# One more sevenfold pair in each of the last two down passes, twice three sevens in a row, and four more weight sums made ahead

## The chip, the cores and the metric

The kernel runs on one core of one Trainium2 chip. The time is device microseconds of one launch; lower is better. The core's engines work from queues of their own and hand over by semaphores: PE (TensorE, matmuls, with its weight loads listed as PEld), DVE (VectorE), ACT (ScalarE), POOL (GpSimd, here almost only an issuer of DMAs), SP (SyncE, an issuer of DMAs).

## The reference, cut to what matters

One decoder layer in float32 for 256 tokens of width 2048: a norm, an RG-LRU branch and a windowed attention branch side by side, gates that merge them, an output projection, and an MLP of width 8192. The change touches the MLP's down projection:

```python
D_MODEL, SEQ, D_FF = 2048, 256, 8192
def rmsnorm(x, g):
    return x * rsqrt(mean(x * x) + 1e-6) * g
# x is the sum of the input and the normed mixer output
u = square(relu(rmsnorm(x, g_mlp_pre) @ w_mlp_up))     # (256, 8192)
y = u @ w_mlp_down                                     # (256, 2048)
out = x + rmsnorm(y, g_mlp_post)
```

## The kernel before, in words

**Products.** PE multiplies in a format (fp32r) that holds less than float32, so each weight and each activation is split into a high part and a low rest. ACT casts (`whi<-wraw`, L108), DVE subtracts (`wlo<-wraw,whi`, L109), and every product is three matmuls, high by high, high by low, low by high (`product`, L1204).

**Weight stream.** All weights come through one stream (class `Stream`). A weight chunk is two halves of 128 x 1024; raw halves are loaded by SP into four slots (five in the MLP, `xraw`), and split into six slots of high and low halves, up to six halves ahead of PE (`AHEAD`). So ACT and DVE work ahead until a slot is missing that PE must free.

**The MLP.** It runs in two halves f = 0, 1 of 4096 inner channels each: an up stage (16 steps), then two down passes n = 0, 1, for the left and the right 1024 output columns. A down pass goes through 16 pairs p of K-blocks. A *plain* pair takes 8 products, so 24 matmuls of 512 columns. A *sevenfold* pair (Strassen's scheme, list `SEVENS`) takes 7, so 21, and in exchange needs sums of weight blocks, T1, T3 and T4, and sums of activation blocks (made once for f, when the up stage hands its block on, four more DVE operations for a pair). The three T sums are split like weights: three casts of 512 columns on ACT (L154, `thi`) and three subtractions on DVE (L155, `tlo`), into three slots each.

**Where the sums come from.** For most sevenfold pairs DVE makes them on the spot from the raw halves (`right_sums`, three operations, L59, L61 and L62, into `t`; they overwrite part of the raw half). For the pairs of `SUMMED` they are made ahead, in earlier stages (`sums_ahead`): POOL loads the chunk in four DMAs of 256 KB (`early<-in_w_dn`, L365), DVE adds, POOL stores the results in three DMAs to a DRAM buffer (`away<-`, L374). In the pass POOL then fetches the three pieces in three DMAs of 256 KB (`second<-away`, L138) into a pool of four slots, and SP loads the raw second half from the DRAM buffer. `gaps` spaces the generator's steps: one step is taken at each half or pair that PE begins.

**The order around it.** Pairs of `SUMS_FIRST` run their three T products first, others last. The T parts of a pair are put into ACT's and DVE's queues one sevenfold pair later than its halves. The pass of f = 1, n = 1 ends with the folds of the output; it has a gain `g3` to multiply into the accumulators, in `between(p)`, four operations of 512 columns. In the pass f = 1, n = 0 the last sevenfold pair's banks are folded into tiles `t` after its products (L1253 to L1257), and the pass ends with four folds `acc<-d..,t` (L1374), which wait for PE.

Of the kernel before, what the change touches and what calls it, by code (L numbers as in the profile page):

```python
# [35 lines left out]

WRAW, WHALF, T2, HELD = 4, 6, 8, 4

SEVENS = (0, 1, 3, 4, 6, 7, 9, 10, 12, 13), (0, 1, 3, 4, 6, 7, 9, 10, 12)
SUMMED = (4, 7, 10, 13), (4, 7, 10)  # L40
SUMS_FIRST = (0, 3, 6, 9, 12)
PAIRS = 16


# [160 lines left out]
def layer(tc, x, few, kx_first, kx_rest, pos_row, gains, w_q, w_xy, w_rg, w_g, w_rp, w_ap, w_out,  # L205
# [155 lines left out]
    def sums_ahead(c, gaps, rooms):  # L361

        w = flat(unit("early", F32))
        for i in range(4):
            nc.gpsimd.dma_start(w[:, quarter(i)], chunks[c][:, quarter(i)])  # L365
            for _ in range(gaps[0]):
                yield
        for _ in range(gaps[1]):
            yield
        one, two = rooms()  # L370
        right_sums(nc.vector, w[:, 0:1024], w[:, 1024:2048], one, two)
        to, b = ws.summed[c]
        for away, of in ((b, w[:, 1024:2048]), (to[:, 0:1024], one), (to[:, 1024:1536], two)):
            nc.gpsimd.dma_start(away, of)  # L374
            for _ in range(gaps[2]):
                yield
# [508 lines left out]
    for m in range(4):  # L885
        recur(m)
        if m == 0:
            pump(99)
            ctx_ps.close()
            psg = ctx1.enter_context(tc.tile_pool(name="psg", bufs=2, space=bass.MemoryType.PSUM))  # L890
            pairs.append(ctx1.enter_context(tc.tile_pool(name="psa2", bufs=1, space=bass.MemoryType.PSUM)))
        if m < 2:
            for i in range(2):
                attn_proj(2 * m + i)
        if m < 3:
            gates(m)
# [24 lines left out]

    ahead = [g_rnn()]
    gates(3)
    ws.side += [sums_ahead(c, (1, 3, 1), unit_rooms) for c in summed[:6]]
    ahead.append(g_rnn())
    for n in range(4):
        gs = ahead.pop(0)
# [193 lines left out]
    for tb in range(TB):  # L1121
        for i in range(2):
            q = 2 + i
# [93 lines left out]
    def down(f, n, uT, held, order, finish, early, between=lambda p: None, behind=lambda: None, closing=False):  # L1217

        two = [pair(f"s{i}") for i in range(2)]
        banks = {name: two[i // 2][:, i % 2].rearrange("p a b -> p (a b)")  # L1220
                 for i, name in enumerate(("P1", "P6", "Q5", "N7"))}
        banks.update((name, bank(psb, f"d{name}")) for name in ("P2", "Q3", "Q4", "Cs"))
        begun = set()
        v = nc.vector

        def step(p, i, hi, lo, name, at=0, w=512, into=None):
            tb, n2 = name
            b = into or PLACE[name]
            o = 0 if into else at
            t = slice(tb * P, tb * P + P)  # L1230
            c = slice(n2 * 512 + at, n2 * 512 + at + w)
            a = uT[p][:, i]
            product(banks[b][:, o : o + w], (a[:, 0, t], a[:, 1, t]), (hi[:, c], lo[:, c]), b in begun,
                    p == PAIRS - 1 and i == 1, w < 512 and not into)
            begun.add(b)

        ready = {}
        for p in range(PAIRS - held - closing):
            if p in SEVENS[f]:
                parts = ws.seven()  # L1240
                names = list(LEFT)
                names.sort(key=lambda name: ("T1", "T3", "T4").index(LEFT[name][1]) if LEFT[name][1] in ("T1", "T3", "T4")
                           else 9 if p in SUMS_FIRST else -1)
                for name in names:
                    i, w = LEFT[name]
                    product(banks[name], left(uT[p], i), parts[w], name in begun,
                            p == SEVENS[f][-1] and (name in ("P1", "P6", "Q5", "N7") or closing and name == PLACE[order[-1]]))
                    begun.add(name)
                if p == SEVENS[f][-1]:
                    for name in ((1, 0), (0, 0), (1, 1), (0, 1)):  # L1250
                        ready[name] = u2("t")
                    x = ready[0, 0]
                    nc.scalar.copy(ready[1, 0], banks["P1"])  # L1253
                    v.tensor_tensor(x, banks["P6"], ready[1, 0], ALU.add)
                    v.tensor_tensor(ready[1, 1], banks["Q5"], x, ALU.subtract)
                    v.tensor_tensor(x, x, banks["N7"], ALU.subtract)
                    v.tensor_tensor(ready[0, 1], ready[1, 1], banks["N7"], ALU.add)  # L1257
                    early(ready)
            else:
                for i in range(2):  # L1260
                    hi, lo = ws.half()
                    for name in order:
                        step(p, i, hi, lo, name)
            between(p)
        parts = []
        if closing:
            for i in range(2):
                parts.append((PAIRS - held - 1, i) + ws.half())
                for name in order[:2]:
                    step(*parts[i], name)  # L1270
        first = len(parts)
        parts += [(p, i) + ws.half(False) for p in range(PAIRS - held, PAIRS) for i in range(2)]
        behind()
        begun.discard("P1")
        for k, name in enumerate(order):
            todo = parts[first if k < 2 else 0 :]
            b, t = banks[PLACE[name]], ready[name]
            if closing and k == 1:
                a, r = order[-1], slice(256, 512)
                fold = lambda: pin(v.tensor_tensor(ready[a][:, r], banks[PLACE[a]][:, r], ready[a][:, r], ALU.add))  # L1280
                for e in todo:
                    step(*e, name)
                finish(name, b, t, 0, 512, fold)
            elif closing and k == 3:
                for e in todo:
                    step(*e, name, 0, 256)
                finish(name, b, t, 0, 256)
                for e in todo:
                    step(*e, name, 256, 256, "P1")
                finish(name, banks["P1"], t, 256, 256)  # L1290
            else:
                for e in todo:
                    step(*e, name)
                finish(name, b, t, 0, 512)
        ws.ahead(ws.at - 1)

    for f in range(2):
        uT = {}
        rooms = []
        if f:  # L1300
            ws.side += [sums_ahead(c, (1, 5, 1), ws.sums_rooms) for c in summed[10:]]
        full = []
        for p in range(PAIRS):
            u = u2("u")
            if f == 0 and p == 1:
                ws.side += [sums_ahead(c, (1, 4, 1), lambda: ws.sums_rooms()) for c in summed[6:10]]
            if f == 0 and p < 2:
                up_pair(p, wide(u))
            else:
                a_pair(h2T, wide(u), PRIO if p == PAIRS - 1 else 0)  # L1310
            full.append((p, u))
            if f == 0 and p == R2_AT:
                pump(99)
                spread_r2()
                ctx3.close()
                pc = ctx2.enter_context(tc.tile_pool(name="pc", bufs=1))
                ws.room = u2
                ws.more = lambda: pc.tile([P, 1024], F32, tag="xraw", name="xraw")
                ws.sums_room = lambda tag: pc.tile([P, 512], F32R, tag=tag, bufs=3, name=tag)
                ws.sums_rooms = lambda: [pc.tile([P, n], F32, tag=f"t{n}", name=f"t{n}") for n in (1024, 512)]  # L1320
            if f == 1 or p >= R2_AT:
                for q, u in full:
                    if q % 2 == 0:
                        rooms.append(unit(f"uT{f}{q}"))
                    room = rooms[-1][:, 2 * (q % 2) : 2 * (q % 2) + 2]
                    if q in SEVENS[f]:
                        three = pc.tile([P, 2, 3, P], F32R, tag="three", bufs=len(SEVENS[0]), name=f"three{f}{q}")
                        uT[q] = three, flat(room).rearrange("p (a b c) -> p a b c", a=2, b=4)
                    else:
                        uT[q] = room  # L1330
                    evacuate(f, q, u, uT[q])
                full.clear()
# [26 lines left out]
        def between(p):  # L1359
            if p < 4:  # L1360
                c = quarter(p)
                nc.sync.dma_start(g3[:, c], gains[3][c].partition_broadcast(P))
            if p in (2, 5, 8, 11):
                tb, q = divmod(p // 3, 2)
                c = quarter(q)
                nc.vector.tensor_tensor(acc[tb][:, c], acc[tb][:, c], g3[:, c], ALU.mult)

# [121 lines left out]
```

## Time and profile before

| what | us |
|---|---|
| median of 3 runs (lowest, highest) | 1488.99 (1488.8, 1489.45) |
| the profiled execution's own time | 1488.93 |
| its span | 1487.0 |
| PE busy | 1477.6 (99%) |
| DVE busy | 1144.4 (77%) |
| ACT busy | 854.8 (57%) |
| POOL busy | 77.5 (5%) |

The span is what the trace covers; the time of a run is 1.9 us longer than it. Busy shares are means over stages with different limits. In the trace the second half's up stage lies at about 1139 to 1317 us, its first down pass at 1317 to 1398 and its second at 1398 to 1480. A wait that the views name by a tile and a line is put down to the operation that released it.

### The profile page before, as it was taken

The page shows a single profiled execution, that of the slowest core. Times are in us where ns is not written, and L with a number is a line of the kernel's source. Part 1 is how long each engine was busy: PE and PEld are TensorE (multiplying, and loading weights), DVE is VectorE, ACT ScalarE, POOL GpSimd, SP SyncE. Part 2 cuts the span into 40 slices and gives each one's busy share as a digit, 9 for nine tenths or more (in the row PEclk, how much of TensorE's full clock was granted, in tenths as well). Part 3 has the DMA queues.
Part 4 walks back from the last instruction along what each step waited for, and adds up shares of the span by engine and source line. Part 5 has one row for each costly group of instructions (what it writes and reads, how often), then busy time and mean ns, then how long its engine had stood idle before and what let it go on. Part 6 is the DMA issues. An engine that isn't in the chain of part 4 may idle for free.

```text
span 1487.0 us, 20528 instructions
## 1 busy us (share of the span) xinstructions
PE 1477.6 (99%) x7556; PEld 1253.4 (84%) x7556; DVE 1144.4 (77%) x1503; ACT 854.8 (57%) x1236; POOL 77.5 (5%) x149
## 2 busy tenths in 40 slices
PE   9999999999999999999999999999999999999997
PEld 8887788888889888888889888888888888888886
DVE  6676668759668867665767888798997777699997
ACT  8564565647467665444355665566564545566563
POOL 0000000000000001110000111000111110000000
PEclk9999999999999999999999999999999999999999
DMA  9654543455646567887864987567788686587674
GB/s 342 229 167 143 174 167 135 171 193 174 208 156 214 185 222 249 310 285 244 310 227 162 321 298 272 181 244 252 268 286 307 225 286 222 200 287 251 198 274 171
DMA packets 96902, 342.38 MB, mean 230 GB/s; under 512 B 11553, under 2 KB 11809, under 8 KB 95777
## 3 DMA queue, kind: packets, MB, share of 16 engines
q1 hardware_dynamic: 80352, 288.89, 57.3%
q0 software_dynamic: 12992, 44.05, 8.4%
q10 hardware_dynamic: 3456, 8.13, 1.5%
q8 instruction: 59, 0.97, 0.3%
q14 instruction: 43, 0.34, 0.1%
HBM read 316.38 MB, written 24.64 MB: 229 GB/s over the span
## 4 chain that ended last, share of the span: by engine, by line
PE 97%; DVE 1%; ACT 1%; DMA 0%; issue 0%; DVEq 0%; ACTq 0%
PE ps L296 22%; PE ps L294 11%; PE dQ L1204 8%; PE s L1204 7%; PE dP L1204 4%; PE g L334 4%; PE g L336 4%; PE pp L334 4%; PE g L338 4%; PE pp L336 4%; PE pp L338 4%; PE dCs L1204 2%; PE q L334 2%; PE q L338 2%; PE q L336 2%; PE o L336 2%
## 5 line engine op out<-in xcount | busy, mean ns | idle before, releaser
L109 DVE TENSOR_TENSOR wlo<-wraw,whi 128x1024 fp32r<-128x1024 f32 x469 | 566.6, 1220 | 245.4 <-ACT whi L108 242.9
L108 ACT CAST whi<-wraw 128x1024 fp32r<-128x1024 f32 x469 | 489.9, 1051 | 452.4 <-PE ps L296 92.9
L296 PE MATMUL ps<-h2T,whi 128*128 128x512 f32 x960 | 223.9, 390 | 0.0
L296 PEld LDWEIGHTS ps<-h2T,whi 128*128 128x128 f32 x960 | 178.2, 188 | 35.7
L294 PEld LDWEIGHTS ps<-h2T,wlo 128*128 128x128 f32 x960 | 119.1, 192 | 2.3
L296 PE MATMUL ps<-hT,whi 128*128 128x512 f32 x512 | 120.6, 391 | 0.0
L294 PE MATMUL ps<-h2T,wlo 128*128 128x256 f32 x960 | 119.9, 283 | 0.0
L296 PEld LDWEIGHTS ps<-hT,whi 128*128 128x128 f32 x512 | 94.7, 188 | 19.5 <-issue 0.7
L1204 PE MATMUL dQ<-whi,uT 128*128 128x512 f32 (+1 forms) x284 | 104.1, 385 | 0.0
L334 PE MATMUL g<-whi,hT 128*128 128x512 f32 x256 | 101.0, 395 | 0.0
L338 PE MATMUL g<-whi,hT 128*128 128x512 f32 x256 | 99.7, 389 | 0.0
L336 PE MATMUL g<-wlo,hT 128*128 128x512 f32 x256 | 99.7, 389 | 0.0
L108 ACT CAST whi<-xraw 128x1024 fp32r<-128x1024 f32 x47 | 49.4, 1052 | 40.7 <-PE ps L296 18.4
L109 DVE TENSOR_TENSOR wlo<-xraw,whi 128x1024 fp32r<-128x1024 f32 x47 | 57.3, 1219 | 12.1 <-ACT whi L108 11.2
L294 PEld LDWEIGHTS ps<-hT,wlo 128*128 128x128 f32 x512 | 63.7, 191 | 2.1 <-issue 0.8
L294 PE MATMUL ps<-hT,wlo 128*128 128x256 f32 x512 | 64.6, 283 | 0.0
L365 POOL DMA_DIRECT2D early<-in_w_dn x56 | 30.4, 543 | 651.9 <-DVE px L324 497.6
L1204 PEld LDWEIGHTS dQ<-whi,uT 128*128 128x128 f32 x284 | 53.0, 188 | 10.6
L334 PEld LDWEIGHTS g<-whi,hT 128*128 128x128 f32 x256 | 48.1, 188 | 10.5 <-issue 1.0
L338 PEld LDWEIGHTS g<-whi,hT 128*128 128x128 f32 x256 | 48.0, 188 | 10.2
L336 PEld LDWEIGHTS g<-wlo,hT 128*128 128x128 f32 x256 | 48.1, 188 | 9.4
L1204 PE MATMUL dQ<-wlo,uT 128*128 128x512 f32 (+1 forms) x142 | 54.6, 385 | 0.0
(309 smaller groups left out, 2744.9 us busy)
## 6 DMA issues: line engine op xcount, KB each, us to landing
wraw<-in_w_up SPq DMA_DIRECT2D x106, 512.0 KB, 4.5
wraw<-in_w_dn SPq DMA_DIRECT2D x93, 512.0 KB, 5.0
wraw<-in_w_g SPq DMA_DIRECT2D x64, 512.0 KB, 4.7
wraw<-in_w_xy SPq DMA_DIRECT2D x64, 512.0 KB, 3.9
wraw<-in_w_q SPq DMA_DIRECT2D x32, 512.0 KB, 4.1
wraw<-in_w_ap SPq DMA_DIRECT2D x32, 512.0 KB, 3.9
wraw<-in_w_rp SPq DMA_DIRECT2D x32, 512.0 KB, 5.3
wraw<-in_w_out SPq DMA_DIRECT2D x32, 512.0 KB, 4.4
```

The costliest lines, as they stand in the source:

```text
L108: self.pin(self.nc.scalar.copy(hi, src))
L109: self.latest_low = self.pin(self.nc.vector.tensor_tensor(lo, src, hi.bitcast(F32), ALU.subtract))
L294: mm(ps[:, f, 1, :], w, a[:, 0, :], start=False, stop=j == 1 and k == 7)
L296: mm(ps[:, f].rearrange("p a b -> p (a b)"), w, a.rearrange("p a b -> p (a b)"), start=kt == 0, stop=j == 3 and k == 7)
L334: mm(banks[tb][n], a[:, 0, t], hi[:, n * 512 : n * 512 + 512], start=first, stop=False)
L336: mm(banks[tb][n], a[:, 0, t], lo[:, n * 512 : n * 512 + 512], start=False, stop=False)
L338: mm(banks[tb][n], a[:, 1, t], hi[:, n * 512 : n * 512 + 512], start=False, stop=last)
L365: nc.gpsimd.dma_start(w[:, quarter(i)], chunks[c][:, quarter(i)])
L1204: mm(b, a[x], w[y], start=not begun and i == 0, stop=tail and i == 2, skip_group_check=shared)
```

## The change

In the second half (f = 1) both passes get ten sevenfold pairs, not nine: 0, 1, 3, 4, 5, 7, 8, 9, 11, 12, so that 3-4-5 and 7-8-9 stand in a row, where before no more than two did. Of them 4, 5, 8, 9 and 12 take sums made ahead (before: 4, 7, 10), and 0, 3, 7 and 11 run their T products first. So 18 chunks have sums made ahead, not 14. The first two are made at the attention projections, the next six where six were made before (beside the recurrence's projections), five in the first half's up stage (before four) and five in the second half's up stage (before four), with shorter gaps between the steps. The four multiplies by `g3` are taken at p = 2, 6, 6 and 10 (before 2, 5, 8 and 11). The host's layout of the weight follows `SEVENS`. The program has 6 matmuls fewer, 16 more operations of two tensors on DVE, 7 more casts on ACT, 40 more DMAs on POOL, and as many DMAs on SP as before.

```diff
--- before.py
+++ after.py
@@ -36,9 +36,9 @@
 
 WRAW, WHALF, T2, HELD = 4, 6, 8, 4
 
-SEVENS = (0, 1, 3, 4, 6, 7, 9, 10, 12, 13), (0, 1, 3, 4, 6, 7, 9, 10, 12)
-SUMMED = (4, 7, 10, 13), (4, 7, 10)
-SUMS_FIRST = (0, 3, 6, 9, 12)
+SEVENS = (0, 1, 3, 4, 6, 7, 9, 10, 12, 13), (0, 1, 3, 4, 5, 7, 8, 9, 11, 12)
+SUMMED = (4, 7, 10, 13), (4, 5, 8, 9, 12)
+SUMS_FIRST = (0, 3, 6, 9, 12), (0, 3, 7, 11)
 PAIRS = 16
 
 
@@ -890,6 +890,7 @@
             psg = ctx1.enter_context(tc.tile_pool(name="psg", bufs=2, space=bass.MemoryType.PSUM))
             pairs.append(ctx1.enter_context(tc.tile_pool(name="psa2", bufs=1, space=bass.MemoryType.PSUM)))
         if m < 2:
+            ws.side.append(sums_ahead(summed[m], (2, 3, 1), unit_rooms))
             for i in range(2):
                 attn_proj(2 * m + i)
         if m < 3:
@@ -921,7 +922,7 @@
 
     ahead = [g_rnn()]
     gates(3)
-    ws.side += [sums_ahead(c, (1, 3, 1), unit_rooms) for c in summed[:6]]
+    ws.side += [sums_ahead(c, (1, 3, 1), unit_rooms) for c in summed[2:8]]
     ahead.append(g_rnn())
     for n in range(4):
         gs = ahead.pop(0)
@@ -1240,7 +1241,7 @@
                 parts = ws.seven()
                 names = list(LEFT)
                 names.sort(key=lambda name: ("T1", "T3", "T4").index(LEFT[name][1]) if LEFT[name][1] in ("T1", "T3", "T4")
-                           else 9 if p in SUMS_FIRST else -1)
+                           else 9 if p in SUMS_FIRST[f] else -1)
                 for name in names:
                     i, w = LEFT[name]
                     product(banks[name], left(uT[p], i), parts[w], name in begun,
@@ -1298,12 +1299,12 @@
         uT = {}
         rooms = []
         if f:
-            ws.side += [sums_ahead(c, (1, 5, 1), ws.sums_rooms) for c in summed[10:]]
+            ws.side += [sums_ahead(c, (1, 3, 1), ws.sums_rooms) for c in summed[13:]]
         full = []
         for p in range(PAIRS):
             u = u2("u")
             if f == 0 and p == 1:
-                ws.side += [sums_ahead(c, (1, 4, 1), lambda: ws.sums_rooms()) for c in summed[6:10]]
+                ws.side += [sums_ahead(c, (1, 3, 1), lambda: ws.sums_rooms()) for c in summed[8:13]]
             if f == 0 and p < 2:
                 up_pair(p, wide(u))
             else:
@@ -1360,8 +1361,8 @@
             if p < 4:
                 c = quarter(p)
                 nc.sync.dma_start(g3[:, c], gains[3][c].partition_broadcast(P))
-            if p in (2, 5, 8, 11):
-                tb, q = divmod(p // 3, 2)
+            for k in {2: (0,), 6: (1, 2), 10: (3,)}.get(p, ()):
+                tb, q = divmod(k, 2)
                 c = quarter(q)
                 nc.vector.tensor_tensor(acc[tb][:, c], acc[tb][:, c], g3[:, c], ALU.mult)
```

How the instructions stand now. First DVE in the pass f = 1, n = 0, from the T parts of pair 4 on; halves 474 and 475 are pair 5's, 476 and 477 pair 6's, 478 and 479 pair 7's. Before:

```order
L109 TENSOR_TENSOR wlo475_12066<-xraw_11980,whi475_12065 128x1024
L155 TENSOR_TENSOR tlo_12093<-second_12017,thi_12092 128x512
L155 TENSOR_TENSOR tlo_12097<-second_12018,thi_12096 128x512
L155 TENSOR_TENSOR tlo_12101<-second_12019,thi_12100 128x512
L59 TENSOR_TENSOR t1024_12104<-wraw477_12031,wraw476_11982 128x1024
L61 TENSOR_TENSOR wraw477_12031<-t1024_12104,wraw476_11982 128x512
L62 TENSOR_TENSOR t512_12105<-wraw477_12031 128x512
L109 TENSOR_TENSOR wlo476_12110<-wraw476_11982,whi476_12109 128x1024
L109 TENSOR_TENSOR wlo477_12114<-wraw477_12031,whi477_12113 128x1024
L155 TENSOR_TENSOR tlo_12143<-t1024_12104,thi_12142 128x512
L155 TENSOR_TENSOR tlo_12147<-t1024_12104,thi_12146 128x512
L155 TENSOR_TENSOR tlo_12151<-t512_12105,thi_12150 128x512
```

and now:

```order
L109 TENSOR_TENSOR wlo475_12123<-xraw_12045,whi475_12122 128x1024
L155 TENSOR_TENSOR tlo_12164<-second_12082,thi_12163 128x512
L155 TENSOR_TENSOR tlo_12168<-second_12083,thi_12167 128x512
L155 TENSOR_TENSOR tlo_12172<-second_12084,thi_12171 128x512
L109 TENSOR_TENSOR wlo476_12176<-wraw476_12047,whi476_12175 128x1024
L109 TENSOR_TENSOR wlo477_12180<-wraw477_12096,whi477_12179 128x1024
L155 TENSOR_TENSOR tlo_12209<-second_12112,thi_12208 128x512
L155 TENSOR_TENSOR tlo_12213<-second_12113,thi_12212 128x512
L155 TENSOR_TENSOR tlo_12217<-second_12114,thi_12216 128x512
L59 TENSOR_TENSOR t1024_12220<-wraw479_12126,wraw478_12098 128x1024
L61 TENSOR_TENSOR wraw479_12126<-t1024_12220,wraw478_12098 128x512
L62 TENSOR_TENSOR t512_12221<-wraw479_12126 128x512
```

Pair 6 was a sevenfold pair with sums on the spot and is now plain; between it and pair 7 stand the T parts of pair 5, made from fetched pieces, and the sums on the spot have moved to pair 7.

POOL at the head of the same pass; the number in `away1536...` is the chunk, 236 for pair 4, 237 for pair 5, 240 for pair 8. Before:

```order
L138 DMA second_12017<-away1536236_85 128x512
L138 DMA second_12018<-away1536236_85 128x512
L138 DMA second_12019<-away1536236_85 128x512
L138 DMA second_12154<-away1536239_87 128x512
L138 DMA second_12155<-away1536239_87 128x512
L138 DMA second_12156<-away1536239_87 128x512
L138 DMA second_12291<-away1536242_89 128x512
```

and now:

```order
L138 DMA second_12082<-away1536236_85 128x512
L138 DMA second_12083<-away1536236_85 128x512
L138 DMA second_12084<-away1536236_85 128x512
L138 DMA second_12112<-away1536237_87 128x512
L138 DMA second_12113<-away1536237_87 128x512
L138 DMA second_12114<-away1536237_87 128x512
L138 DMA second_12270<-away1536240_89 128x512
```

The second set of three follows for the pair just behind the first, where before it was for a pair three further on; the slots are four as before.

DVE at the turn from n = 0 to n = 1 of the second half: halves 498 and 499 are pair 1's of the new pass, and `acc0<-dCs` is the last fold of the old one, which waits for PE. Before:

```order
L1374 TENSOR_TENSOR acc1_11919<-dP2_11924,t_12497 128x512
L1374 TENSOR_TENSOR acc0_11918<-dQ4_11926,t_12498 128x512
L59 TENSOR_TENSOR t1024_12629<-wraw499_12518,wraw498_12474 128x1024
L1374 TENSOR_TENSOR acc0_11918<-dCs_11927,t_12500 128x512
L61 TENSOR_TENSOR wraw499_12518<-t1024_12629,wraw498_12474 128x512
L1366 TENSOR_TENSOR acc0_11918<-acc0_11918,g3_12654 128x512
L62 TENSOR_TENSOR t512_12630<-wraw499_12518 128x512
L109 TENSOR_TENSOR wlo498_12635<-wraw498_12474,whi498_12634 128x1024
L109 TENSOR_TENSOR wlo499_12639<-wraw499_12518,whi499_12638 128x1024
```

and now:

```order
L1375 TENSOR_TENSOR acc1_11984<-dP2_11989,t_12578 128x512
L59 TENSOR_TENSOR t1024_12710<-wraw499_12599,wraw498_12555 128x1024
L1375 TENSOR_TENSOR acc0_11983<-dQ4_11991,t_12579 128x512
L61 TENSOR_TENSOR wraw499_12599<-t1024_12710,wraw498_12555 128x512
L1367 TENSOR_TENSOR acc1_11984<-acc1_11984,g3_12735 128x512
L62 TENSOR_TENSOR t512_12711<-wraw499_12599 128x512
L1375 TENSOR_TENSOR acc0_11983<-dCs_11992,t_12581 128x512
L109 TENSOR_TENSOR wlo498_12716<-wraw498_12555,whi498_12715 128x1024
L109 TENSOR_TENSOR wlo499_12720<-wraw499_12599,whi499_12719 128x1024
```

The two folds ahead stand apart, and the last one has moved behind the second and third operation of the sums and behind the multiply by `g3`, so that the low half follows it at once.

## The prediction

> **What bounds the kernel now.** I read the page's head first, then the chain of work that ended last, then what TensorE waits for, then the two passes of the second half in the chain.
>
> ```profile
> span 1487.0 us, 20528 instructions
> PE 1477.6 (99%) x7556; PEld 1253.4 (84%) x7556; DVE 1144.4 (77%) x1503; ACT 854.8 (57%) x1236; POOL 77.5 (5%) x149
> PE 97%; DVE 1%; ACT 1%; DMA 0%; issue 0%; DVEq 0%; ACTq 0%
> PE warm L440 <- DVE ones L424: 1.1, 1, 1.1
> PE kv L476 <- ACT hT L460: 0.4, 1, 0.4
> PE pt L693 <- DVE s L677: 0.2, 1, 0.2
> ```
>
> PE is busy 99% of the span, carries 97% of the chain, and its whole list of waits is three lines, 1.7 us, none of them in the MLP. So time can leave this kernel by fewer matmuls or by the tail, and can come in wherever a piece of weight reaches PE late. The chain gives the price of one matmul (start, length, work):
>
> ```profile
> 978.82 1.36 PE s L1204 x6
> 993.78 1.36 PE s L1204 x6
> ...
> 1398.03 1.36 PE s L1204 x6
> 1428.08 1.36 PE s L1204 x6
> ```
>
> The first two rows are the starts of two successive triples "seven, seven, plain" in the first half: 21 + 21 + 24 = 66 matmuls in 993.78 - 978.82 = 14.96 us, so 0.2267 us each; a seven lasts 4.76 us, a plain pair 5.44 us, one product of three matmuls 0.68 us. The last two rows span two such triples at the head of the second half's second pass: 30.05 us, where 132 x 0.2267 = 29.92. So that pass loses 0.13 us at its head in stalls too short for the list of waits.
>
> ```profile
> 1317.00:1398.00 81.00, 81.00 (x359) 67.08 (x358) 73.26 (x87) 50.03 (x67) 3.76 (x7) 1.00 0.79 266
> 1398.00:1480.00 82.00, 81.31 (x376) 67.69 (x374) 76.65 (x99) 46.40 (x68) 4.30 (x8) 1.00 0.65 226
> 1327.00:1337.00 10.00, 10.00 (x46) 8.28 (x45) 9.37 (x12) 7.92 (x12) 0.00 (x0) 1.00 1.04 389
> 1337.00:1347.00 10.00, 10.00 (x46) 8.29 (x45) 9.93 (x13) 6.19 (x8) 1.61 (x3) 1.00 0.88 288
> 850.00:960.00 110.00, 110.00 (x634) 97.38 (x633) 85.69 (x111) 63.03 (x80) 9.22 (x17) 1.00 0.76 261
> ```
>
> These rows are busy times by stretch: window, length, PE, PE loads, DVE, ACT, POOL, granted clock, DMA share, GB/s. The two passes to be changed are the first two rows. DVE is at 90 to 93% there, the next engine to bind; the granted clock is 1.00 throughout, so it is no term.
>
> **The change part by part.**
>
> *Sevenfold pairs.* One more seven in each of two passes: 3 matmuls fewer in each, 6 in all, at 0.2267 = **-1.36 us**, on the path, since PE is the chain. All else has to be shown hidden.
>
> *DVE's work in the passes* (start, length, work):
>
> ```profile
> 1336.39 1.89 DVE L155 TENSOR_TENSOR tlo<-second,thi 128x512 fp32r<-128x512 f32 x3
> 1338.19 1.22 DVE L59 TENSOR_TENSOR t<-wraw,wraw 128x1024 f32<-128x1024 f32 x1
> ...
> 1340.78 2.35 DVE L109 TENSOR_TENSOR wlo<-wraw,whi 128x1024 fp32r<-128x1024 f32 x2
> L155 DVE TENSOR_TENSOR tlo<-second,thi 128x512 fp32r<-128x512 f32 x18 | 11.3, 682 | 0.0
> L154 ACT CAST thi<-second 128x512 fp32r<-128x512 f32 x18 | 10.1, 618 | 0.0
> ```
>
> A plain pair costs DVE 2.35 us, a seven with sums made ahead 2.35 + 1.89 = 4.24, a seven that adds its sums on the spot another 1340.78 - 1338.19 = 2.59, so 6.83. A triple before takes 6.83 + 4.24 + 2.35 = 13.42 of PE's 14.96 us. The new quadruple (on the spot, ahead, ahead, plain) takes 6.83 + 4.24 + 4.24 + 2.35 = 17.66 of PE's 3 x 4.76 + 5.44 = 19.72. The share is the same 90%: DVE doesn't become the bound by its sum. Of the sums on the spot a pass has six before and five after, of the T splits nine and ten: 1.89 - 2.59 = -0.7 us of DVE per pass, less work than now.
>
> *What gets tight: the pieces of two summed pairs in a row.* Each summed pair fetches three 256 KB pieces by POOL's queue into a pool of four slots. Pair 4's three and pair 5's first fill it; pair 5's second piece (T3) is issued only when pair 4's first piece has been split by DVE. These issues in the trace, first pass then second, and what follows each: how long it took to land (minimum, median, maximum).
>
> ```profile
> 1337.48 1.78 POOL L138 DMA_DIRECT2D second<-away  x3 [13.88 <-DVE tlo L155]
> DMA to landing us min/median/max: 5.3/5.4/5.4
> 1350.49 1.14 POOL L138 DMA_DIRECT2D second<-away  x2 [11.24 <-DVE tlo L155]
> DMA to landing us min/median/max: 6.4/6.4/6.5
> 1420.25 1.74 POOL L138 DMA_DIRECT2D second<-away  x3 [19.62 <-DVE tlo L155]
> DMA to landing us min/median/max: 5.5/5.5/5.5
> 1434.05 1.14 POOL L138 DMA_DIRECT2D second<-away  x2 [12.06 <-DVE tlo L155]
> DMA to landing us min/median/max: 7.1/7.1/7.2
> 1341.43 0.39 PE L1204 MATMUL dQ<-whi,uT 128*128 128x512 f32 x1
> ```
>
> The last row is the first matmul of pair 5 in the first pass; pair 4 so began at 1341.43 - 4.76 = 1336.67. Pair 5 will run T1, T3, T4 last: T3 begins 4.76 + 5 x 0.68 = 8.16 us after pair 4's start, and its low part is read one matmul later, 8.39. Before that lie ACT's cast (0.62) and DVE's subtraction (0.68); for the two hand-overs I allow 0.15. So a piece may take 8.39 - 1.45 = 6.94 us to land, less the time by which its issue follows the start of the pair ahead.
> - First pass, pair 5: issue 0.81 after pair 4's start: 6.13 allowed, 5.4 seen, 0.7 to spare.
> - Second pass, pair 5: pair 4 starts at 1428.08 - 5.44 - 4.76 = 1417.88, so the issue at 1420.25 is 2.37 late: 4.57 allowed, 5.5 seen. Alone that would be 0.9 us of stall. But pair 12 of the first pass, now with sums made ahead, runs its T products last, so the slots of its halves come free three products (2.04 us) sooner, which is what ACT and, behind it, DVE wait for there; and in DVE's order the three ops that stood between the last bank's fold and the next low half are now ahead of that fold:
>
> ```profile
> 1398.25 0.68 DVE L1374 TENSOR_TENSOR acc<-dCs,t 128x512 f32<-128x512 f32 x1
> 1400.66 2.35 DVE L109 TENSOR_TENSOR wlo<-wraw,whi 128x1024 fp32r<-128x1024 f32 x2
> ```
>
> The fold waits for PE's end of the pass; the low half followed 2.41 us later, and can now follow 0.6 later: 1.8 us sooner, on an engine that runs without a break from there on. I take this: 6.4 allowed, 0.9 to spare, and the 0.13 us at the pass's head goes too, **-0.1 us**. If DVE does not come sooner, 0.9 of stall is the other end.
> - Second pass, pair 9: its pieces wait for pair 8, as those issued at 1434.05 waited for pair 7, which began at 1428.08 + 4.76 = 1432.84: 1.21 late, 5.73 allowed; half of the 1.8 as what remains of it by then: 6.6. Seen were 5.5 to 7.1: between nothing and 0.5 of stall; I take **+0.2 us**.
> - First pass, pair 9: pair 7 began at 1341.43 + 4.76 + 5.44 = 1351.63, the issue at 1350.49 was 1.14 ahead: 8.1 allowed, 6.4 seen, hidden.
>
> Behind pair 5's waiting subtraction on DVE stand the sums, low halves and T parts of pair 7 (6.83 us). First pass: the pieces end their split at about 1345.1, pair 7's first T part 2.59 + 2.35 + 0.68 later, 1350.7; PE needs it at 1341.43 + 4.76 + 5.44 = 1351.6. Hidden, with 0.9 to spare, and a late piece delays PE as well.
>
> *Four more sums ahead: 40 POOL DMAs more (28 loads and stores, 12 pieces) and 4 x 2.59 us of DVE in earlier stages.* Cost taken: nothing. Two stand in the attention projections:
>
> ```profile
> 272.10 1.75 PE L693 MATMUL pt<-ident,s 128*128 128x128 f32 x14 [0.25 <-DVE s L677]
> 287.25 1.23 DVE L109 TENSOR_TENSOR wlo<-wraw,whi 128x1024 fp32r<-128x1024 f32 x1 [3.34 <-ACT whi L108]
> 380.91 1.23 DVE L109 TENSOR_TENSOR wlo<-wraw,whi 128x1024 fp32r<-128x1024 f32 x1 [2.62 <-ACT whi L108]
> 297.22 1.22 DVE L109 TENSOR_TENSOR wlo<-wraw,whi 128x1024 fp32r<-128x1024 f32 x1 [1.49 <-ACT whi L108]
> 299.94 1.22 DVE L109 TENSOR_TENSOR wlo<-wraw,whi 128x1024 fp32r<-128x1024 f32 x1 [1.50 <-ACT whi L108]
> L365 POOL DMA_DIRECT2D early<-in_w_dn x56: 536/538/676, 500.0 to 1212.7; - x56
> DMA to landing us min/median/max: 3.3/7.4/10.3
> ```
>
> The first falls into the 3.34 us for which DVE stands idle before 287.25 and fits it (2.59). Its loads can start when the transposes end, 273.85, the fourth is issued by 276.0 and lands by 283.4 (median) to 286.3 (longest); DVE gets there at 283.9. At the longest the low half behind it comes 286.3 + 2.59 - 287.25 = 1.6 us late, and halves are split up to six ahead, each 2.7 us of PE (297.22 to 299.94): covered. The second stands near the 2.62 us idle ahead of 380.91, which it fills. The other two lie in the MLP's up halves, where DVE is busy 85.69 of 110 us and one sum is 2.59. If all four lost their cover: 10.4 us; nothing in these rows says so. The gap from the last load to the sum is one or two halves shorter there than before; a DVE wait for a load would first use up the halves that lie ready.
>
> *The rest.* Four more evacuations on DVE in the second half's up (under 1.3 us each by its ops above, with the same cover), the g3 multiplies at other places of the last pass (as many as before, 0.68 us each like the fold at 1398.25), SP's queue with the same number of DMAs: no term. Of PE's tail nothing changes.
>
> Sum: the profiled run took 1488.93 us for a span of 1487.0 (the 1.93 around it stays), 0.06 under the median of 1488.99. 1488.93 - 1.36 - 0.1 + 0.2 = 1487.67, **1487.6 us** for the median of runs.
>
> **Two rules weighed.** The 42 issues of the pieces:
>
> ```profile
> L138 POOL DMA_DIRECT2D second<-away x42: 536/536/552, 963.6 to 1434.7; - x42
> DMA to landing us min/median/max: 2.9/5.5/7.2
> ```
>
> They took 536 to 552 ns each, most in stretches where DVE is over 90% busy. The Trainium skill, "SBUF — State Buffer", section "SBUF: two separate sides", has DVE and GpSimd share a port pair as an exclusive lock, which a DVE op with two SBUF inputs takes only against a GpSimd op that reads SBUF. By that, an issue stuck behind one DVE op would take up to 1.2 us more and every late place above would be 1.2 us tighter; the spread of 16 ns shows no such wait. The Trainium skill, "DMA: Bandwidth & Descriptors", section "Where 436 GB/s comes from", gives about 358 GB/s as HBM's share of one core; with the quadruple's pieces 1337:1347 would move some 288 + 79 = 367 (up to three pieces of 256 KB more in 10 us). By that limit this stretch would be saturated and the pieces would land as late as any seen; the row of 389 GB/s above, which counts all that the engines moved, shows the queues going past that figure for 10 us, with PE at 10.00 of 10.00.
>
> **The rivals.**
> 1. *The pieces land as late as any of the 42* (7.2 us), since two summed pairs in a row put more on the queues at once: 7.2 - 6.13, - 6.4 and - 6.6 are 1.1 + 0.8 + 0.6 = 2.5 us: 1487.47 + 2.5 = 1490.0, within 0.2% of now. For it: those after busy stretches (1434.05) did take 7.1. Against: 1337.48, the very place, took 5.4.
> 2. *Slower, by the second pass's late start:* DVE does not come 1.8 us sooner (because raw weights or ACT's casts hold it), and the pieces are at 7.2 as well. Pair 5 then stalls 7.2 - 4.57 = 2.6, pair 9 7.2 - 5.73 = 1.5, first pass 1.1: 5.2 us, 1488.93 - 1.36 + 5.2 = 1492.8. It decides from 4.4 us of stalls, that is with landings from 6.9 us on when nothing comes sooner, or 7.9 when it does. Against it: the two DVE rows, and that the longest landing is 7.2 in these passes. For it: 10.3 was seen on the same queue.
> 3. *Faster by over 0.2%* would take 3 us. With 1.36 of matmuls and 0.13 of short stalls there is 1.49; the rest would have to come from the chain's 3% outside PE, at the kernel's ends, which the change does not touch. Best case 1487.4.
> 4. *The hidden DVE sums are not hidden* (attention projections): one at 1.6 us late or more past its cover, 1489 to 1491.
>
> **How the numbers follow.** I call 0.2% (3.0 us, 1486.0 to 1492.0) about what a measurement of this kernel can tell from no change. Pieces in time or nearly, 1487.0 to 1488.4: 0.64. Rival 1: 0.17, rival 4 inside the 0.2%: 0.05. Slower (rival 2, or rival 4 several times over): 0.11. Faster: 0.03. So same 0.86. The range reaches from 1487.0 (all in time, run spread 0.4) to 1490.4 (rival 1 with its spread); above it lie 0.13, below it about 0.05.
>
> **What would show it.** Right: a quadruple 19.7 us long in the chain, PE's list of waits still without an MLP line, the issues for pair 5 about 1337.5 and 1418 landing under 6.2 us, second pass without the 0.13. Wrong: a wait of PE for `tlo` or `thi` in a pair 5 or 9 (rivals 1, 2), DVE's idle time before `tlo` put down to `second`, or a wait in the projections around 288 or 381 (rival 4).

## The result, and the profile after

| | median us | lowest to highest | runs |
|---|---|---|---|
| kernel before | 1489.36 | 1488.64 to 1489.82 | 15 |
| kernel after | 1493.21 | 1490.4 to 1495.07, without the first | 15 |

The kernel after is slower: ratio 1.0024, 95% interval 1.0016 to 1.0032. The prediction was 1487.6 us, at most 1490.4. The first execution of the kernel after, the profiled one, ran at a granted clock of 0.556 and took 2483.51 us; it counts in the median (1493.14 without it) and is left out of everything else. The profile shown is of the same kernel run once more: 1492.49 us median of 8, ratio 1.0023, interval 1.0013 to 1.0033. Its profiled execution took 1494.12 us and is the slowest of these eight, so the losses read from it lie some 1.6 us above those of a median run. The spread is new: 4.7 us from the fastest to the slowest, where the kernel before has 1.2 here and at most 2.0 beside the experiments.

The head of the page, and the largest of PE's waits (us in total, times, longest):

```profile
span 1492.2 us, 20651 instructions
PE 1479.6 (99%) x7550; PEld 1252.3 (84%) x7550; DVE 1155.5 (77%) x1519; ACT 856.7 (57%) x1243; POOL 99.2 (7%) x189
PE s L1205 <- DVE tlo L155: 1.2, 3, 0.8
PE s L1205 <- ACT thi L154: 1.2, 2, 0.6
PE warm L440 <- DVE ones L424: 1.1, 1, 1.1
PE dQ L1205 <- DVE tlo L155: 0.6, 3, 0.2
```

The 6 matmuls are gone. In their place stand three lines that the list of before did not have: PE waits for the T parts, 3.0 us in all (a fourth, of 0.2 us, is of an up stage). Stalls of a fraction of a microsecond between matmuls are not in that list. The starts of each pair's first matmul show them all: what a pair takes beyond 21 or 24 times 0.2267 us, in this execution,

| pass | pair | lost us |
|---|---|---|
| first (n = 0) | 9 | 0.8 |
| second (n = 1) | 1 | 1.1 |
| | 3 | 0.1 |
| | 5 | 2.0 |
| | 9 | 2.1 |

and nothing above 0.05 us at any other pair: 6.2 us in the two passes, where the kernel before loses 0.13. 1488.93 - 1.36 + 6.2 = 1493.8, beside 1494.12 measured. So all of the loss but 0.3 us lies in the two passes: at pair 9 of both, at pair 5 of the second, and at pair 1, that is at the turn between the passes.

DVE in the first pass, and ACT's casts of pair 5's three pieces (start, length, work, idle time before it and what ended it):

```profile
1338.63 2.35 DVE L109 TENSOR_TENSOR wlo<-wraw,whi 128x1024 fp32r<-128x1024 f32 x2
1341.45 0.69 DVE L155 TENSOR_TENSOR tlo<-second,thi 128x512 fp32r<-128x512 f32 x1 [0.47 <-ACT thi L154]
1344.26 1.37 DVE L155 TENSOR_TENSOR tlo<-second,thi 128x512 fp32r<-128x512 f32 x2 [2.11 <-ACT thi L154]
1345.55 1.22 DVE L59 TENSOR_TENSOR t<-wraw,wraw 128x1024 f32<-128x1024 f32 x1
...
1356.75 1.89 DVE L155 TENSOR_TENSOR tlo<-second,thi 128x512 fp32r<-128x512 f32 x3
1340.80 0.62 ACT L154 CAST thi<-second 128x512 fp32r<-128x512 f32 x1 [1.68 <-PE s L1205]
1343.61 1.30 ACT L154 CAST thi<-second 128x512 fp32r<-128x512 f32 x2 [2.19 <-DMA second<-away]
```

At pair 5 DVE stands still for 0.47 + 2.11 = 2.6 us, with pair 7's sums behind it in its queue. Each time it waits for ACT's cast: the first cast had waited for PE, which by the order frees its slot; the second, behind which stands the longer wait, for the fetched piece. PE loses nothing at pair 5. But DVE comes to pair 8's T parts only at 1356.75, 39.3 us after the start of the pass (1317.48; without the wait it is 37.2, as the kernel with one pair mended will show), and with them comes the issue of pair 9's second piece. The same is then seen at the turn:

```profile
1357.84 0.54 POOL L138 DMA_DIRECT2D second<-away  x1 [11.28 <-DVE tlo L155]
DMA to landing us min/median/max: 6.2/6.2/6.2
...
L86 SPq DMA_DIRECT2D wraw<-in_w_dn x2: 327/328/328, 1374.4 to 1375.6; - x2
DMA to landing us min/median/max: 5.9/6.0/6.1
1380.42 1.05 ACT L108 CAST whi<-wraw 128x1024 fp32r<-128x1024 f32 x1 [2.90 <-PE s L1205]
...
1401.30 0.69 DVE L1375 TENSOR_TENSOR acc<-dCs,t 128x512 f32<-128x512 f32 x1
1401.89 2.35 DVE L109 TENSOR_TENSOR wlo<-wraw,whi 128x1024 fp32r<-128x1024 f32 x2
```

A raw load issued at 1374.4 lands 6.0 us later, at 1380.4, and ACT casts that half at 1380.42 (the profile puts the wait down to PE, which had long been done). The load could not go earlier: in this stretch SP's queue waits for DVE's low halves alone, and DVE ends one at 1374.4 (begun at 1373.18, 1.22 us). So DVE's lateness goes round by way of the raw loads to the casts and back to DVE. The low half of the next pass's pair 1 follows the fold at once (0.6 us), as the order says, but the fold itself stands at 1401.30, 2.8 us after PE went over to the new pass at 1398.53.

### The profile page after: what moved, and what is told of

It is laid out like the page before. It is cut to its first block, busy times and chain, and to the rows that moved or that the text cites. A ratio compares the mean times of both kernels' runs of the same rounds, so it can differ in the third digit from the quotient of the medians.

```text
span 2481.4 us, 20651 instructions
## 1 busy us (share of the span) xinstructions
PE 2472.3 (100%) x7550; PEld 1568.9 (63%) x7550; DVE 1179.3 (48%) x1519; ACT 871.9 (35%) x1243; POOL 99.2 (4%) x189
## 4 chain that ended last, share of the span: by engine, by line
PE 99%; DMA 0%; DVE 0%; ACT 0%; DVEq 0%; issue 0%
PE ps L296 23%; PE ps L294 11%; PE dQ L1205 8%; PE s L1205 8%; PE dP L1205 4%; PE g L334 4%; PE g L338 4%; PE pp L336 4%; PE pp L338 4%; PE pp L334 4%; PE g L336 4%; PE dCs L1205 2%; PE q L336 2%; PE q L334 2%; PE q L338 2%; PE o L336 2%
## 5 line engine op out<-in xcount | busy, mean ns | idle before, releaser
L296 PE MATMUL ps<-h2T,whi 128*128 128x512 f32 x960 | 375.3, 576 | 0.0
L296 PE MATMUL ps<-hT,whi 128*128 128x512 f32 x512 | 201.0, 577 | 0.0
L294 PEld LDWEIGHTS ps<-h2T,wlo 128*128 128x128 f32 x960 | 187.4, 271 | 10.6 <-issue 5.7
L294 PE MATMUL ps<-h2T,wlo 128*128 128x256 f32 x960 | 190.1, 383 | 0.0
L334 PE MATMUL g<-whi,hT 128*128 128x512 f32 x256 | 149.2, 583 | 0.0
L1205 PE MATMUL dQ<-whi,uT 128*128 128x512 f32 (+1 forms) x272 | 149.2, 569 | 0.0
L338 PE MATMUL g<-whi,hT 128*128 128x512 f32 x256 | 147.5, 576 | 0.0
L336 PE MATMUL g<-wlo,hT 128*128 128x512 f32 x256 | 147.2, 575 | 0.0
L294 PEld LDWEIGHTS ps<-hT,wlo 128*128 128x128 f32 x512 | 99.9, 269 | 7.3 <-issue 4.4
L294 PE MATMUL ps<-hT,wlo 128*128 128x256 f32 x512 | 102.2, 383 | 0.0
L1205 PE MATMUL s<-thi,uT 128*128 128x512 f32 x160 | 83.9, 574 | 0.0
```

What stands on the lines that cost most here:

```text
L294: mm(ps[:, f, 1, :], w, a[:, 0, :], start=False, stop=j == 1 and k == 7)
L296: mm(ps[:, f].rearrange("p a b -> p (a b)"), w, a.rearrange("p a b -> p (a b)"), start=kt == 0, stop=j == 3 and k == 7)
L334: mm(banks[tb][n], a[:, 0, t], hi[:, n * 512 : n * 512 + 512], start=first, stop=False)
L336: mm(banks[tb][n], a[:, 0, t], lo[:, n * 512 : n * 512 + 512], start=False, stop=False)
L338: mm(banks[tb][n], a[:, 1, t], hi[:, n * 512 : n * 512 + 512], start=False, stop=last)
L1205: mm(b, a[x], w[y], start=not begun and i == 0, stop=tail and i == 2, skip_group_check=shared)
```

## The experiments

Times are medians of all runs of a kernel; what pairs lose is from its profiled execution, worked out as above.

**The changed kernel once more, and its parts taken apart.**

> The changed kernel once more, unaltered, for a trace at full clock. Theory A (pieces late: the T pieces of pairs 5 and 9 come after PE has reached them): PE waits for tlo or thi in pair 5 and pair 9 of the second half's passes, together 4 to 6 us; the time is 1491 to 1495 us, 2 to 6 above before. Theory B (the cover of the sums made ahead is gone): PE waits near 288 or 381 us or in the up stages, and the two passes last what their matmuls cost.

1492.49 us, and the waits are those for `tlo` and `thi` shown above: 4.9 us at pairs 5 and 9, and 1.1 us at the turn, which theory A had not named. Nothing near 288 or 381. Theory A.

```diff
-SUMMED = (4, 7, 10, 13), (4, 5, 8, 9, 12)
-SUMS_FIRST = (0, 3, 6, 9, 12), (0, 3, 7, 11)
+SUMMED = (4, 7, 10, 13), (4, 5, 8, 9)
+SUMS_FIRST = (0, 3, 6, 9, 12), (0, 3, 7, 11, 12)
...
-            ws.side.append(sums_ahead(summed[m], (2, 3, 1), unit_rooms))
```

> One part undone: no sums at the attention projections; pair 12 makes its sums on the spot again and runs its T products first, so 16 chunks have sums made ahead; the pairs 3-4-5 and 7-8-9 stay. Theory A: the loss stays and pair 5 of the second pass gets worse by up to 1.8 us, since the turn between the passes is again as in the kernel before: 1492 to 1497 us. Theory B: most of the loss goes, 1487.5 to 1489 us.

1499.5 us, ratio 1.0069 (1.0053 to 1.0086): beyond theory A's range on the far side from B.

```profile
PE s L1204 <- ACT thi L154: 4.6, 4, 1.4
PE s L1204 <- DVE tlo L155: 1.2, 4, 0.4
```

Pair 9 loses 0.8 and 2.9 us, pair 5 of the second pass 2.0, no more than in the kernel after, and pairs 11 and 12, which now both make their sums on the spot, lose 2.9 in each pass. That I had not reckoned: two pairs of 6.83 us of DVE in a row ask 13.66 of a DVE that has 2 x 4.76 = 9.52 us of PE time for them.

```diff
+    extra = [len(chunks) - 32 + i for i in (1, 3, 6, 9)]
...
+            ws.side.append(sums_ahead(extra[m], (2, 3, 1), unit_rooms))
...
-            ws.side += [sums_ahead(c, (1, 5, 1), ws.sums_rooms) for c in summed[10:]]
+            ws.side += [sums_ahead(c, (1, 3, 1), ws.sums_rooms) for c in extra[3:] + summed[10:]]
```

(and the like in the first half's up stage, on the kernel before)

> The kernel before with one part of the change alone: four more sums are made ahead and stored (two at the attention projections, one in each half's up stage with the shorter gaps), and nobody reads them; the passes stay as before. Theory A: no cost, 1489 to 1490 us. Theory B: the whole loss of 3 to 4 us plus the 1.4 us that the change takes away, 1493 to 1495 us.

1489.04 us, ratio 1.0 (0.999 to 1.0009). The sums made ahead cost nothing. DVE at the first of the new places:

```profile
284.00 1.22 DVE L59 TENSOR_TENSOR early_t<-early 128x1024 f32<-128x1024 f32 x1
285.25 0.69 DVE L61 TENSOR_TENSOR early<-early_t,early 128x512 f32<-128x512 f32 x1
285.98 0.69 DVE L62 TENSOR_TENSOR early_t<-early 128x512 f32<-128x512 f32 x1
287.42 1.23 DVE L109 TENSOR_TENSOR wlo<-wraw,whi 128x1024 fp32r<-128x1024 f32 x1 [0.75 <-ACT whi L108]
```

The 3.34 us of idle time have become 2.59 of work and 0.75 idle, and the low half behind them is where it was. This settles theory B and the prediction's fourth rival.

```diff
         if summed:
-            pieces = [self.room("second") for _ in range(3)]
+            if j // 2 in self.in_t:
+                one, two = self.sums_rooms()
+                pieces = [one[:, 0:512], one[:, 512:1024], two]
+            else:
+                pieces = [self.room("second") for _ in range(3)]
```

(`in_t` holds the chunks of pairs 5 and 9 of the second half's two passes)

> The changed kernel, but the pieces of pairs 5 and 9 are fetched into the two tiles in which the sums on the spot are made, not into the pool of four slots; so their loads start when the pair before the last has been split, some 5 us sooner. Theory A: the waits at pairs 5 and 9 go and the time falls to 1487 to 1488.5 us. Theory B: it stays at 1491 to 1495 us.

1487.62 us, and no pair loses more than 0.03. POOL in the first pass and the landings of the pieces that go to the other room:

```profile
1330.95 1.70 POOL L143 DMA_DIRECT2D t<-away  x3 [7.33 <-DVE tlo L160]
1337.13 1.74 POOL L143 DMA_DIRECT2D second<-away  x3 [4.48 <-DVE tlo L160]
...
DMA to landing us min/median/max: 4.1/5.3/6.6
```

Pair 5's pieces are issued at 1330.95, not 1337.9, behind pair 3's T parts; the three at 1337.13 are pair 8's. With the slots taken away as a cause, the loss is gone whole, at the turn too.

**Where it starts, and how it is carried.**

The other room is given to fewer pairs, in each of three kernels by one of the three lines:

```diff
-    ws.in_t = {len(chunks) - 32 + 16 * n + p for n in range(2) for p in (5, 9)}
+    ws.in_t = {len(chunks) - 32 + p for p in (5, 9)}
+    ws.in_t = {len(chunks) - 16 + p for p in (5, 9)}
+    ws.in_t = {len(chunks) - 32 + 5}
```

> The other room for pairs 5 and 9 in the second half's first pass only; the second pass fetches into the pool of four as the change has it. Theory A (one wait in the first pass makes DVE late, and that lateness is carried through the raw loads into the second pass): the first pass loses nothing, nor does pair 1 of the second pass (1.1 us lost there now); pair 4's T parts come about 0.7 us after pair 4's start and not 2.4, so pair 5 loses 0 to 0.8 us and pair 9 0 to 1.5: 1487.6 to 1489.9 us. Theory C (each pass loses what its own pieces cost): the 4 us of pairs 5 and 9 of the second pass stay, 1491 to 1493 us.

> The other room for pairs 5 and 9 in the second pass only. Theory A: the first pass keeps its loss at pair 9 (0.8 us) and the second its loss at pair 1 (about 1.1 us), the 4 us at pairs 5 and 9 of the second pass go: 1489.2 to 1490 us. Theory C: only the 0.8 us are left, 1488.2 to 1488.6 us.

> The other room for one pair alone, pair 5 of the first pass. Theory A (DVE's 2.6 us of waiting at pair 5 is what makes the pieces of pair 9 late and the turn too): pair 9 of the first pass loses nothing although its pieces still come through the pool of four, and the time is that of the first-pass kernel, 1487.6 to 1489.9 us. Theory D (pair 9's pieces are late by themselves, since they land in 6 us and more): the 0.8 us at pair 9 and the loss at the turn stay, 1491 to 1493 us.

| kernel | median us, ratio (interval) | profiled execution | first pass loses | second pass loses |
|---|---|---|---|---|
| other room in the first pass | 1490.06, 1.0004 (0.9995 to 1.0014) | 1490.5 | 0 | 2.0 (pair 9) |
| in the second pass | 1489.66, 1.0005 (0.9995 to 1.0014) | 1491.79 | 1.5 (pair 9) | 1.1 (pair 1), 0.2 (3), 1.2 (5) |
| for pair 5 of the first pass | 1490.92, 1.0011 (1.0002 to 1.0021) | 1487.73, the fastest of its ten | 0 | 0.5 (pair 9) |

Theory C falls: with the first pass mended the losses at pairs 1 and 5 of the second pass, 3.1 us, go too, although nothing of the second pass was changed; and with only the second pass mended, pair 5 there loses 1.2 us with its pieces in time. What the second pass loses there is the first's lateness. Pair 9 of the second pass is another matter: its 2.0 us stay with the first pass mended. In the traced execution theory D falls for the first pass: with pair 5 alone mended, pair 9 still fetches through the four slots, and loses nothing.

```profile
1355.01 1.76 POOL L143 DMA_DIRECT2D second<-away  x3 [16.48 <-DVE tlo L160]
DMA to landing us min/median/max: 6.0/6.5/7.4
```

Its pieces are issued 2.8 us sooner than in the kernel after (1355.01 for 1357.84; 2.0 us sooner counted from the start of the pass) and take about as long to land (the three in the kernel after: 6.2 to 7.6 us). But this execution is 3.2 us faster than the median of its kernel, and by the times theory D isn't excluded: 1490.92 lies 1.0 above theory A's range (1489.9) and 0.1 under theory D's, and the first-pass kernel's 1490.06 is 0.2 above A's. Where the slower runs lose their time no trace shows. The kernel `r9_sums_ahead_of_wait` below is the better witness.

The turn of the first of these kernels:

```profile
1398.19 0.69 DVE L1381 TENSOR_TENSOR acc<-dCs,t 128x512 f32<-128x512 f32 x1
1398.80 2.35 DVE L110 TENSOR_TENSOR wlo<-wraw,whi 128x1024 fp32r<-128x1024 f32 x2
```

PE went over to the new pass at 1397.99, and DVE is there. The 1.8 us that the prediction counted on are real when nothing was lost before.

> The kernel with the other room for pairs 5 and 9 in both passes once more, to measure how much faster it is than the kernel before. By its matmuls (1.36 us) and the 0.13 us that the second pass loses in the kernel before: 1.5 us faster, ratio 0.9990; if some cover elsewhere is thin, up to 0.9997.

1487.74 us (1487.33 to 1488.19), ratio 0.9991, interval 0.9982 to 1.0. With the earlier runs that is 21 of this kernel from 1486.9 to 1488.47, as even as the kernel before; 1.4 us less, which is the six matmuls and hardly more. Its interval just reaches no change. It is the fastest of all that was run.

**Is it DVE's standing still, or the late piece?**

```diff
             one, two = self.sums_rooms()
             right_sums(v, a, b, one, two, self.keep)
+            self.settle()
...
-        self.begin()
+        self.begin(self.at // 2 in self.hold)
         j = self.at
         self.at += 2
         self.ahead(j)
+        self.settle()
```

(`begin` leaves out its `settle` where told to hold: at pairs 5 and 9 of the two passes)

> The changed kernel with one reordering and no other slots: in DVE's queue the three sums that pairs 7 and 11 make on the spot stand ahead of the T parts of pairs 5 and 9, not behind, so DVE does 2.6 us of work in the time for which it now stands and waits for the pieces. The pieces come by the same pool of four. Theory A (what hurts is the 2.6 us that DVE stands still in a stretch that has 2.1 us to spare): the loss at the turn and most of that at pair 9 goes, at pairs 5 and 9 up to 0.7 us each can remain since a piece is no earlier: 1487.6 to 1490 us. Theory E (the pieces themselves come too late, whatever DVE does meanwhile): the loss stays above 3 us, 1490.5 to 1493.5 us.

1488.95 us, ratio 0.9999 (0.999 to 1.0009): 3.5 us of the changed kernel's time gone by an order on DVE alone, with the pieces through the same four slots. The profiled execution (1488.63 us) is close to the median, and in it pair 9 loses nothing in either pass, so theory D falls for the first pass here too.

```profile
1340.14 1.22 DVE L59 TENSOR_TENSOR t<-wraw,wraw 128x1024 f32<-128x1024 f32 x1
1341.39 0.69 DVE L61 TENSOR_TENSOR wraw<-t,wraw 128x512 f32<-128x512 f32 x1
1342.12 0.69 DVE L62 TENSOR_TENSOR t<-wraw 128x512 f32<-128x512 f32 x1
1342.73 2.06 DVE L157 TENSOR_TENSOR tlo<-second,thi 128x512 fp32r<-128x512 f32 x3
```

The sums fill what was the wait, and the pieces are there when DVE comes. One loss is left in the profiled execution, 1.05 us at pair 5 of the second pass, more than the 0.7 allowed. There the sums themselves are held up, by a raw load and a multiply by `g3` between them, and the T parts behind them follow late:

```profile
1421.69 1.23 DVE L59 TENSOR_TENSOR t<-wraw,xraw 128x1024 f32<-128x1024 f32 x1 [0.76 <-DMA wraw<-in_w_dn]
1422.83 0.69 DVE L1372 TENSOR_TENSOR acc<-acc,g 128x512 f32<-128x512 f32 x1
...
1424.76 1.89 DVE L157 TENSOR_TENSOR tlo<-second,thi 128x512 fp32r<-128x512 f32 x3
```

Theory E falls. The 1.2 us that remain to the kernel with the other room are this loss, as far as one execution shows it.

**One place left.**

```diff
-    ws.in_t = {len(chunks) - 32 + 16 * n + p for n in range(2) for p in (5, 9)}
+    ws.in_t = {len(chunks) - 32 + i for i in (5, 9, 16 + 5)}
```

> The other room for pairs 5 and 9 of the first pass and pair 5 of the second; pair 9 of the second pass still fetches into the pool of four, and its loss there was 2.0 us in the trace of the first-pass kernel. Theory A: with no wait at pair 5, pair 8's T parts and the fetch behind them come about 2 us sooner, and pair 9 loses 0 to 0.5 us: 1487.6 to 1488.4 us. Theory D (pair 9's pieces land in 7 to 8 us and are late by that): the 2 us stay, 1489.5 to 1490.2 us.

1488.78 us median, ratio 0.9997 (0.9988 to 1.0006), between the two ranges; 1487.44 to 1490.36, and the profiled execution is the fastest of the ten and loses nothing. So with no wait at pair 5, pair 9 can be in time through the four slots. The median lies about 1.1 us over the kernel with the other room throughout; that could be theory D's in the slower runs, but the profiled execution doesn't show it.

```profile
1435.82 1.77 POOL L143 DMA_DIRECT2D second<-away  x3 [16.47 <-DVE tlo L160]
DMA to landing us min/median/max: 6.8/7.5/8.4
```

Set beside each other, the traces that have pair 9 of the second pass on the four slots show what decides there. The second column counts from the pass's first matmul and leaves out what PE had lost in the pass by then:

| kernel | issue of pair 9's second piece, us into the pass | the three landings, us | pair 9 loses |
|---|---|---|---|
| after | 40.8 | 6.9 to 8.4 | 2.1 |
| other room in the first pass | 40.8 | 6.8 to 8.4 | 2.0 |
| other room for pair 5 of the first pass | 40.9 | 5.6 to 6.8 | 0.5 |
| sums ahead of the wait | 38.2 | 6.8 to 7.5 | 0 |
| other room at three places | 38.6 | 6.8 to 8.4 | 0 |

With the same landings the loss is 2.0 us or nothing, by an issue some 2.2 us sooner; and at the late issue the landing makes 0.5 or 2.0 of it. So the wait at pair 5 takes the cover away, and how long the pieces then take to land sets the price.

## Why the prediction was wrong

It named the place, the pieces of two summed pairs through four slots, and it had the kernel's time in its second rival (1492.8 us at a chance of 0.11), but it forecast that the place would hold. Its own figure of 1487.6 us (its sum gives 1487.67) is what the kernel with the other room takes (1487.62 and 1487.74), in which the wait that it left out is not there. By its steps:

- **Six matmuls, -1.36 us: right.** The kernel with the other room, in which no pair loses time, is 1.4 us under the kernel before.
- **The sums made ahead at no cost: right** (1489.04 beside 1489.0 with them alone).
- **First pass, pair 5, 0.7 us to spare: right.** Issue 1337.91, landing 5.6 to 6.3 us, no loss.
- **"DVE doesn't become the bound by its sum": the step that failed.** 17.66 of 19.72 us counted DVE's work and not its waiting. At pair 5 the prediction had DVE wait for the piece, and followed the delay as far as pair 7's T parts, where 0.9 us were to spare. But 17.66 + 2.6 of standing still is 20.3, more than the quadruple's 19.72: the delay does not die out, it is handed on. In the trace DVE takes 19.93 us from pair 4's T parts (1336.82) to pair 8's (1356.75), less than that sum since operations in a row overlap a little, but more than the quadruple; without the wait at pair 5 it takes 18.2.
- **First pass, pair 9, 8.1 us allowed, hidden: wrong by that.** The issue was put 1.14 us ahead of the start of the pair ahead, as with pair 7 in the kernel before; in the new order that is pair 8. It came 0.9 us behind pair 8's start (1357.84 beside 1356.9). Without the wait at pair 5 it was 1.1 ahead of that start, as predicted (1355.01 beside 1356.1). The loss was 0.8 us.
- **The turn, 1.8 us sooner: wrong in the kernel after, right without the wait.** The order allowed it (0.6 us between the fold and the low half, as worked out), but DVE came to the fold 2.8 us late, by way of the raw loads. Pair 1 lost 1.1 us where I had put -0.1.
- **Second pass, pairs 5 and 9, 0 and 0.2 us: wrong,** 2.0 and 2.1. Of pair 5 it was the turn; of pair 9 the wait at pair 5 once more, and a landing longer than the "5.5 to 7.1" that it had:

```profile
1442.61 1.75 POOL L138 DMA_DIRECT2D second<-away  x3 [11.27 <-DVE tlo L155]
DMA to landing us min/median/max: 6.9/7.6/8.4
```

- **The second rival** had "nothing comes sooner" and landings of 7.2 us: 5.2 us of stalls, of which 2.6 at pair 5, 1.5 at pair 9 and 1.1 in the first pass. Measured 6.2 in the profiled execution, 2.0, 2.1 and 0.8, and 1.2 at pairs 1 and 3, so its total came close in part by luck. Its condition was held to be a mishap of raw weights or casts from outside; it is a consequence of the first pass's wait.
- **The chances.** The range ended at 1490.4, and 0.86 stood on no change by the 0.2% bound. The median of 1493.21 lies beyond it, past the bound of 1492.0. The first rival, all pieces at 7.2 us, was priced place by place, as though a late piece cost only its own lateness.
- Of the two rules weighed, the lock of the Trainium skill, "SBUF — State Buffer", section "SBUF: two separate sides", had no part in it: the issues of the pieces in these two passes took 536 to 546 ns in the kernel after. The other, the limit of some 358 GB/s of the Trainium skill, "DMA: Bandwidth & Descriptors", section "Where 436 GB/s comes from", was passed in the kernel before with PE at full work (389 GB/s in 1327:1337). The loss came in stretches of 315 to 346 GB/s, where PE waited:

```profile
1357.00:1367.00 10.00, 9.78 (x43) 7.46 (x41) 6.39 (x9) 4.61 (x6) 2.69 (x5) 1.00 0.94 346
1440.00:1450.00 10.00, 9.60 (x43) 7.62 (x41) 6.38 (x8) 3.39 (x5) 2.16 (x4) 1.00 0.91 315
```

## What to carry to other kernels

Add an engine's waits in its queue to its work before calling it unbound: one in-order wait that cost PE nothing where it stood cost the next consumers, in a stretch that wait and work together exceeded. Follow a delay through the slots that the delayed engine frees (here raw loads and fetches) until it meets a place where the engine is idle by more than the delay, and not only to the next consumer. Here the wait was mended for the most part by putting work that is ready ahead of it, which needs no room, and wholly by giving the late transfer a room that comes free sooner.

## What the runs showed of the hardware

The pieces' landing time isn't a property of their size. Fetches of the same 256 KB took 3.0 to 7.2 us in these two passes of the kernel before, and up to 8.4 in the kernel after. Nor does a late landing need an engine that was held up: at about the same place of the second pass the pieces issued at 1434.05 took 7.1 to 7.2 us in the kernel before, and two issued at 1436.54 took 7.7 to 8.6 in the second run of the kernel with the other room throughout (`r8_other_slots_again`), in both with PE at full work and no loss. So the other room doesn't make the pieces land sooner; it makes them start sooner. The kernel with the first pass mended, ten microseconds from 1438 on, and its raw loads of that time:

```profile
1438.83 1.75 POOL L143 DMA_DIRECT2D second<-away  x3 [11.27 <-DVE tlo L160]
DMA to landing us min/median/max: 6.8/7.5/8.4
DMA packets 986, 3.54 MB, mean 354 GB/s; under 512 B 127, under 2 KB 127, under 8 KB 984
DMA to landing us min/median/max: 7.1/7.9/8.5
```

The raw loads, too, took 7.1 to 8.5 us then, against 5.9 to 6.1 around the like place in the kernel before (1432 to 1437). That both are late for sharing the DMA engines would fit these rows, but in the kernel before the pieces took 7.1 us beside raw loads of 5.9 to 6.1, and no run takes the one away from the other, so it stays open. So does the share of the landing times in the spread of 4.7 us from run to run, which the kernel before (1.2 to 2.0 us) and the one with the other room throughout (1.6 us over its 21 runs) don't have; two traces with the same late issue, 0.5 and 2.0 us of loss, show that they can make some 1.5 us of it.
